# The MLP's down projection as seven block products (Strassen's scheme) in place of eight

## The chip, the cores and the metric

The kernel runs on one core of a Trainium2 chip. The metric is the time of one execution on the device, in microseconds (us). A run of a kernel gives several such times; the median is compared. Beside the times there is a profile of one execution, taken by the hardware profiler, with every instruction's start and length. The engines are TensorE (PE, with its weight loads as PEld), VectorE (DVE), ScalarE (ACT), GpSimd (POOL) and SyncE (SP), which here only issues transfers. Each engine works through its own queue in order and waits on semaphores of the others.

## What is computed

One layer of a streaming encoder on x of 512 tokens x 1024 channels, float32: four parallel token mixers, then cross-attention into 256 memory tokens, then a gated MLP. Only the MLP is touched:

```
hf  = rms_norm(x, norm_ffn_pre)                              # 512 x 1024
u   = dwconv_causal(hf @ w_up, ffn_dw) + ffn_dw_b            # w_up: 1024 x 5632, width-3 taps
u_g, u_v = split(u, 2, axis=-1)                              # 2816 channels each
yff = (silu(u_g) * u_v) @ w_down                             # w_down: 2816 x 1024
x   = x + rms_norm(yff, norm_ffn_post)
```

## The kernel before, in words

Every float32 product is made of three passes. Each operand is split into a high part, rounded to the type that PE multiplies in one pass (float32r), and a low part, the rest; `mm3` issues high x high, high x low, low x high into the same PSUM bank (line 224 is the `PE.matmul` that all of them share). A split is an ACT copy (the high part, L183 for weights, L152 for activations) and a DVE subtraction (the low part, L184 and L153).

Work is a stream of jobs, each a block of weights and a body that uses it. `run_blocks` keeps three jobs ahead: before it runs a body it fetches the next job, that is, it issues the load of the raw weights on SP (`load_raw`, L169, two raw tiles `wr` in turn) and their split into one of four pairs of tiles `wh` and `wl`. A planner then orders the instructions of each engine by a simulated time line, so the order in a queue can differ from the program's; what waits for what follows from the tiles.

Up projection (`up_jobs`): 44 blocks of 128 channels, gate and value block in turn, 24 matmuls each over all 512 tokens. The result lies channel by channel: 128 channels x 512 tokens in one of four PSUM banks (`mm`, `av`). `done` takes it out: scale and bias on ACT (L1286), two taps on DVE (L518), and after the value block the activation silu(gate) * value (L1290 to L1292). Before, that product is split into `ns.act`, a high and a low tile for all 22 channel blocks.

Down projection (`down_jobs`): 22 blocks `kk` of 128 channels. For each, 4 token tiles x 2 halves of the 1024 output columns, three passes each: the 128 x 128 activation is the stationary operand, 512 columns of `w_down` the moving one. The eight results fill the eight PSUM banks. The last four blocks are held back, and then done tile by tile: 12 matmuls close the first half of a token tile, 12 the second. Behind each half come a square with a sum on ACT (L1345) and a product with the gain on DVE (L1348); behind both, the reciprocal root of the mean square on POOL (`rstd_of`, L261 and L264), the residual sum on DVE (L1355) and the store to `out` on SP (L1356).

Of the kernel before, what the change touches and what calls it, by code (L numbers as in the profile page):

```python
# [16 lines left out]
F32 = mybir.dt.float32  # L17
F32R = mybir.dt.float32r
AF = mybir.ActivationFunctionType
ALU = mybir.AluOpType  # L20
# [4 lines left out]
P = 128  # L25
S = 512
D = 1024
NT = S // P
# [5 lines left out]
NF = DFF // P  # L34
EPS = 1e-6
WB = 2 * 520
# [46 lines left out]
def hybrid_layer(ctx: ExitStack, tc: tile.TileContext, a: dict, out: bass.AP):  # L83
    nc = tc.nc
    V, A, G, PE, SP = nc.vector, nc.scalar, nc.gpsimd, nc.tensor, nc.sync


    gp = ctx.enter_context(tc.tile_pool(name="g", bufs=1))
# [7 lines left out]
    def bank(tag=None):  # L96
        if tag is None:
            turn_of.n += 1
            tag = "av" if turn_of.shared and turn_of.n % 2 else "mm"
        return psum.tile([P, 512], F32, tag=tag, name=f"ps_{tag}", bufs=2)  # L100
# [41 lines left out]
    def weights_tile(kind):  # L142

        i = w_used[kind]
        w_used[kind] += 1
        return w_tiles.pop((kind, i), None) or gp.tile([P, WB], F32R, tag=f"{kind}{i % 4}", name=kind)


    def split(ps, hi, lo, scale=None):

        if scale is None:
            A.copy(hi, ps)  # L152
            V.tensor_tensor(lo, ps, hi.bitcast(F32), ALU.subtract)  # L153
        else:
            A.activation(hi, ps, AF.Copy if isinstance(scale, float) else AF.Identity, scale=scale)
            V.scalar_tensor_tensor(lo, ps, scale, hi.bitcast(F32), ALU.mult, ALU.subtract)
# [33 lines left out]
    def cols(w, c0, n=P, k0=0, nk=NK):  # L190

        return w[k0 * P:(k0 + nk) * P, c0:c0 + n].rearrange("(k p) c -> p k c", p=P), [P, nk, n]
# [3 lines left out]
    def run_blocks(jobs, ahead=3):  # L196


        jobs = iter(jobs)
        pending = []  # L200

        def fetch():
            while True:
                job = next(jobs, None)
                if job is None:
                    return
                if job[1] is None:
                    pending.append((job[0] or (), job[2]))
                else:
                    pending.append((load_weights(*job[:2], *job[3:]), job[2]))  # L210
                if job[0] is not None:
                    return

        for _ in range(ahead):
            fetch()
        while pending:
            if pending[0][0]:
                fetch()
            w, body = pending.pop(0)
            body(*w)  # L220
            bg.tick()
# [9 lines left out]
    def mm3(ps, w_hi, w_lo, x_hi, x_lo, first, last):  # L231

        matmul(ps, w_hi, x_hi, first, False)
        matmul(ps, w_hi, x_lo, False, False)
        matmul(ps, w_lo, x_hi, False, last)
# [20 lines left out]
    def rstd_of(pool, parts, n=1):  # L256

        m = pool.tile([P, n], F32, tag="st_m", name="st_m", bufs=4)
        r = pool.tile([P, n], F32, tag="st_r", name="st_r", bufs=4)
        if len(parts) == 2:  # L260
            G.tensor_scalar(m, parts[0], parts[1], EPS, ALU.add, ALU.add)  # L261
        else:
            G.tensor_scalar(m, parts[0], EPS, None, ALU.add)
        G.tensor_tensor(r, m, nhalf[:, :n], ALU.pow)  # L264
        return r
# [21 lines left out]
    def new_ht():  # L287
        if ht_tiles:
            return ht_tiles.pop(0), ht_tiles.pop(0)
        return (gp.tile([P, NK, S], F32R, tag="hth", name="hth"),  # L290
                gp.tile([P, NK, S], F32R, tag="htl", name="htl"))
# [973 lines left out]
            yield *cols(w_xo, b // 2 * 512, 512, b % 2 * 2, 2), body  # L1265


    def open_ffn():
        bg.drain("n1")
        close(ns.work_)  # L1270
        close(ns.xp_)
        close(ns.xm_)
        ns.fp_, ns.fp = new_pool("ffn", False)
        ns.work = ns.fp
        ns.act = (ns.fp.tile([P, NF, S], F32R, name="acth"), ns.fp.tile([P, NF, S], F32R, name="actl"))
        ns.post = ns.fp.tile([P, D], F32, name="g_ffn")
        G.dma_start(ns.post, a["norm_ffn_post"][0].partition_broadcast(P))

    def up_jobs():
        st, held = {}, []  # L1280

        def done(j, i, ps):
            if i == 0:
                st[j] = ns.fp.tile([P, 2, S], F32, tag="c", name="c", bufs=2)
            c, ch = st[j], i * NF + j
            A.activation(c[:, i], ps, AF.Identity, bias=pc("fb", ch), scale=pc("fdw2", ch))  # L1286
            taps(c[:, i], ps, lambda k: pc("fdw01", k * 44 + ch), 3)
            if i == 1:
                th = ns.fp.tile([P, S], F32, tag="th", name="th")
                A.activation(th, c[:, 0], AF.Tanh, scale=0.5)  # L1290
                V.scalar_tensor_tensor(th, th, 1.0, c[:, 0], ALU.add, ALU.mult)
                V.scalar_tensor_tensor(c[:, 1], th, 0.5, c[:, 1], ALU.mult, ALU.mult)  # L1292
                split(c[:, 1], ns.act[0][:, j], ns.act[1][:, j])


        for n in range(2 * NF):
            def body(hi, lo, n=n):
                j, i = divmod(n, 2)
                if n > 3:
                    ps = bank()  # L1300
                    channel_major(ps, (hi, lo), ns.hf)
                    done(j, i, ps)
                    return
                if n == 0:
                    bg.drain("n0")
                ps = bank(("mm", "sc")[n % 2])
                (channel_major if n else by_pass)(ps, (hi, lo), ns.hf, slice(0, S // 2))
                held.append((j, i, ps, (hi, lo)))
                if n == 3:
                    open_ffn()  # L1310
                    for j, i, ps, w in held:
                        (channel_major if i or j else by_pass)(ps, w, ns.hf, slice(S // 2, S))
                        done(j, i, ps)
            yield *cols(w_up, n % 2 * DFF + n // 2 * P), body, V, same, HALF_SHIFT if n < 4 else 0

    def down_jobs():
        tail = 4
        held, ps = [], []

        def step(t, i, kk, hi, lo):  # L1320
            sl, csl = slice(t * P, (t + 1) * P), slice(i * 512, (i + 1) * 512)
            mm3(ps[t][i], ns.act[0][:, kk, sl], ns.act[1][:, kk, sl], hi[:, csl], lo[:, csl], kk == 0, kk == NF - 1)

        for kk in range(NF):
            def body(hi, lo, kk=kk):
                if kk == 0:
                    tags = (("mm", "mm"), ("av", "av"), ("sc", "sc"), ("tr", "tr"))
                    ps.extend([bank(n) for n in pair] for pair in tags)
                if kk < NF - tail:
                    for t in range(NT):  # L1330
                        for i in range(2):
                            step(t, i, kk, hi, lo)
                    return
                held.append((kk, hi, lo))
                if kk < NF - 1:
                    return
                for t in range(NT):
                    res, o = ns.out[t], ns.fp.tile([P, 2, S], F32, tag="c", name="o", bufs=2)
                    ms = []
                    for i in range(2):  # L1340
                        for w in held:
                            step(t, i, *w)
                        ms.append(ns.fp.tile([P, 1], F32, tag=f"pm{i}", name=f"pm{i}", bufs=2))
                        junk = ns.fp.tile([P, S], F32, tag="th", name="junk")
                        A.activation(junk, ps[t][i], AF.Square, scale=1.0 / math.sqrt(D), accum_out=ms[i])  # L1345
                        if i == 1:
                            r = rstd_of(ns.fp, ms)
                        V.tensor_tensor(o[:, i], ps[t][i], ns.post[:, i * 512:(i + 1) * 512], ALU.mult)  # L1348
                    for i in range(2):
                        sl = slice(i * 512, (i + 1) * 512)  # L1350
                        parts = 2 if (t, i) == (NT - 1, 1) else 1
                        for q in range(parts):
                            n = 512 // parts
                            c, d = slice(q * n, (q + 1) * n), slice(sl.start + q * n, sl.start + (q + 1) * n)
                            V.scalar_tensor_tensor(o[:, i, c], o[:, i, c], r, res[:, d], ALU.mult, ALU.add)  # L1355
                            SP.dma_start(out[t * P:(t + 1) * P, d], o[:, i, c])  # L1356
            yield w_down[kk * P:(kk + 1) * P, :], [P, D], body

    def all_jobs():
        yield from mixer_jobs()  # L1360
# [43 lines left out]
```

## Time and profile before

| | |
|---|---|
| median of 3 runs | 1081.77 us (1080.86 to 1082.29) |
| profiled execution | 1081.09 us |
| its span, first to last instruction | 1079.3 us |
| PE busy | 1071.2 us, 99% of the span |
| up projection, the part with all its pools open | 728 to 953 us |
| down projection, first matmul to the last one's end | 953.17 to 1073.03 us |
| end after the last matmul | 6.27 us |
| matmuls in all | 5453 |

Lines of the profile name a group: the line of the kernel, the engine, the operation, what is written `<-` what is read with shapes, the count, the busy time and the mean of one instruction in nanoseconds, and the idle time of that engine just before, with what ended it. Rows of a time line give the start and the length in us first. Matmuls overlap in the pipeline, so their lengths add up to more than the time; their pace is read from their starts.

### The profile page before, as it was taken

The page shows a single profiled execution, that of the slowest core. Times are in us where ns is not written, and L with a number is a line of the kernel's source. Part 1 is how long each engine was busy: PE and PEld are TensorE (multiplying, and loading weights), DVE is VectorE, ACT ScalarE, POOL GpSimd, SP SyncE. Part 2 cuts the span into 40 slices and gives each one's busy share as a digit, 9 for nine tenths or more (in the row PEclk, how much of TensorE's full clock was granted, in tenths as well). Part 3 has the DMA queues.
Part 4 walks back from the last instruction along what each step waited for, and adds up shares of the span by engine and source line. Part 5 has one row for each costly group of instructions (what it writes and reads, how often), then busy time and mean ns, then how long its engine had stood idle before and what let it go on. Part 6 is the DMA issues. An engine that isn't in the chain of part 4 may idle for free.

```text
span 1079.3 us, 14199 instructions
## 1 busy us (share of the span) xinstructions
PE 1071.2 (99%) x5453; PEld 910.7 (84%) x5453; DVE 695.9 (64%) x1131; ACT 465.3 (43%) x785; POOL 104.0 (10%) x189
## 2 busy tenths in 40 slices
PE   9999999999999999999999999999999999999997
PEld 8888888888888988888888899998888888888886
DVE  7899996466666467857464486868666666642224
ACT  5322222467464364654443365645444444431112
POOL 4000001000101033323000120120000000000001
PEclk9999999999999999999999999999999999999999
DMA  6433433332222243233155343134333333333322
GB/s 203 116 98 91 90 107 95 93 98 78 59 81 78 69 127 98 81 96 117 59 176 180 113 146 92 57 99 118 97 98 98 98 98 98 98 98 97 98 78 78
DMA packets 145848, 109.29 MB, mean 101 GB/s; under 512 B 3647, under 2 KB 133292, under 8 KB 145781
## 3 DMA queue, kind: packets, MB, share of 16 engines
q1 hardware_dynamic: 143219, 99.85, 31.1%
q0 software_dynamic: 2560, 8.54, 2.7%
q8 instruction: 43, 0.70, 0.3%
q14 instruction: 24, 0.20, 0.1%
q10 hardware_dynamic: 2, 0.00, 0.0%
HBM read 106.27 MB, written 2.11 MB: 100 GB/s over the span
## 4 chain that ended last, share of the span: by engine, by line
PE 99%; ACT 0%; DVE 0%; POOLq 0%; issue 0%; DVEq 0%; POOL 0%; ACTq 0%
PE ps_mm L224 52%; PE ps_av L224 31%; PE ps_sc L224 8%; PE ps_tr L228 3%; PE ps_tr L224 3%; PE ps_mm L431 1%; PE ps_av L431 1%; PE ps_mm L373 0%; PE ps_sc L378 0%; DVE o L1355 0%; PE ps_tr L415 0%; POOLq L1400 0%; ACT junk L1345 0%; ACT hth L152 0%; ACT hth L421 0%
## 5 line engine op out<-in xcount | busy, mean ns | idle before, releaser
L184 DVE TENSOR_TENSOR wl<-wr,wh 128x1024 fp32r<-128x1024 f32 (+1 forms) x172 | 212.2, 1235 | 194.2 <-ACT wh L183 193.7
L183 ACT CAST wh<-wr 128x1024 fp32r<-128x1024 f32 (+1 forms) x172 | 180.1, 1049 | 318.4 <-PE ps_mm L224 127.8
L224 PE MATMUL ps_mm<-hth,wh 128*128 128x512 f32 (+1 forms) x616 | 231.4, 382 | 0.2 <-ACT hth L152 0.2
L224 PE MATMUL ps_mm<-hth,wl 128*128 128x512 f32 (+1 forms) x616 | 230.0, 380 | 0.0
L224 PE MATMUL ps_mm<-htl,wh 128*128 128x512 f32 (+1 forms) x616 | 229.9, 380 | 0.0
L224 PEld LDWEIGHTS ps_mm<-hth,wh 128*128 128x128 f32 x616 | 114.3, 188 | 21.1 <-ACT hth L152 0.5
L224 PEld LDWEIGHTS ps_mm<-hth,wl 128*128 128x128 f32 x616 | 114.0, 188 | 21.1
L224 PEld LDWEIGHTS ps_mm<-htl,wh 128*128 128x128 f32 x616 | 114.0, 188 | 20.4 <-DVE htl L153 0.2
L224 PE MATMUL ps_av<-hth,wh 128*128 128x512 f32 (+1 forms) x328 | 122.4, 373 | 0.0
L224 PE MATMUL ps_av<-htl,wh 128*128 128x512 f32 (+1 forms) x328 | 122.4, 373 | 0.0
L224 PE MATMUL ps_av<-hth,wl 128*128 128x512 f32 (+1 forms) x328 | 122.3, 373 | 0.0
L584 DVE SCALAR_TENSOR_TENSOR y<-y,par,y 128x499 f32<-128x499 f32 (+28 forms) x120 | 82.3, 729 | 0.2
L224 PEld LDWEIGHTS ps_av<-htl,wh 128*128 128x128 f32 x328 | 61.7, 188 | 10.9
L224 PEld LDWEIGHTS ps_av<-hth,wh 128*128 128x128 f32 x328 | 61.5, 188 | 10.9
L224 PEld LDWEIGHTS ps_av<-hth,wl 128*128 128x128 f32 x328 | 61.5, 188 | 10.8
L224 PE MATMUL ps_mm<-y,wh 128*128 128x512 f32 x192 | 61.2, 394 | 0.0
L261 POOL TENSOR_SCALAR st_m<-pm,pm 128x1 f32<-128x1 f32 x12 | 6.4, 533 | 435.6 <-ACT junk L1345 350.2
L224 PEld LDWEIGHTS ps_mm<-y,wh 128*128 128x128 f32 x192 | 35.4, 188 | 6.8
L152 ACT CAST acth<-c 128x512 fp32r<-128x512 f32 x22 | 13.7, 621 | 56.9 <-DVE c L1292 56.9
L224 PE MATMUL ps_mm<-y,wl 128*128 128x512 f32 x96 | 37.6, 392 | 0.0
L907 POOL TENSOR_SCALAR fbias<-ck,cq 128x128 f32<-128x128 f32 (+3 forms) x32 | 27.6, 868 | 68.0 <-DVE st L913 63.5
L518 DVE SCALAR_TENSOR_TENSOR c<-ps_mm,par,c 128x510 f32<-128x510 f32 (+1 forms) x44 | 32.8, 745 | 0.7
(379 smaller groups left out, 1901.4 us busy)
## 6 DMA issues: line engine op xcount, KB each, us to landing
wr<-in_w_up SPq DMA_DIRECT2D x44, 512.0 KB
wr<-in_w_in SPq DMA_DIRECT2D x38, 512.0 KB
wr<-in_w_gate SPq DMA_DIRECT2D x32, 512.0 KB
wr<-in_w_down SPq DMA_DIRECT2D x22, 512.0 KB
wr<-in_w_branch SPq DMA_DIRECT2D x16, 512.0 KB
wr<-in_w_out SPq DMA_DIRECT2D x8, 512.0 KB
xr<-in_w_xkv SPq DMA_DIRECT2D x8, 512.0 KB
wr<-in_w_in SPq DMA_DIRECT2D x4, 520.0 KB
```

The costliest lines, as they stand in the source:

```text
L152: A.copy(hi, ps)
L183: order(A.copy(hi, raw[:, :n]))
L184: low.tensor_tensor(lo, raw[:, :n], hi.bitcast(F32), ALU.subtract)
L224: PE.matmul(ps, lhs, rhs, start=start, stop=stop)
L228: PE.transpose(ps, x, ident[:n, :n])
L261: G.tensor_scalar(m, parts[0], parts[1], EPS, ALU.add, ALU.add)
L431: keep(PE.matmul(banks[c][:, :S // 2], w[p == 1][:, k, c * P:(c + 1) * P], ht[p == 2][:, i * 4 + k, :S // 2], start=(i, p, k) == (0, 0, 0) ...
L518: V.scalar_tensor_tensor(dst[:, s:], src[:, :S - s], w(k), dst[:, s:], ALU.mult, ALU.add)
L584: V.scalar_tensor_tensor(dst[:, s:], src[:, :S - s], pc("conv_dw", k * 4 + j), dst[:, s:], ALU.mult, ALU.add)
L907: G.tensor_scalar(bias[:, :w], ck[j][:, :w], -1.0, cq[:, qt, head:head + 1], ALU.mult, ALU.add)
```

## The change

The product Y = A B, with A the activations (512 tokens x 2816) and B = `w_down`, is cut into halves in each direction: A by tokens (first and last 256) and by channel blocks (even and odd ones), B by the same channel blocks and by its columns (first and last 512). So a pair `q` of channel blocks (2q, 2q + 1) gives A11, A12, A21, A22 (first index tokens, second even or odd block) and B11, B12, B21, B22, and there are 11 pairs. With Winograd's form of Strassen's scheme:

```
S1 = A21 + A22   S2 = S1 - A11   S3 = A11 - A21   S4 = A12 - S2
T1 = B12 - B11   T3 = B22 - B12  T2 = T3 + B11    N4 = B21 - T2
M1 = A11 B11   M2 = A12 B21   M3 = S4 B22   M4 = A22 N4   M5 = S1 T1   M6 = S2 T2   M7 = S3 T3
Y11 = M1 + M2              Y12 = M1 + M6 + M5 + M3
Y21 = M1 + M6 + M7 + M4    Y22 = M1 + M6 + M7 + M5
```

Each M sums over the 11 pairs in PSUM: 256 tokens x 512 columns, two banks.

- During the up projection, `weight_pair` (POOL's transfers) brings the two `w_down` blocks of a pair, `weight_sums` forms T3, T1, T2 and N4 on DVE in place, and POOL stores them in the DRAM tile `sums`. One pair comes every three blocks, from the seventh block on. The tiles are `dw`, four in turn.
- The activation is no longer split in the up projection. It is kept in float32 in `ns.quart[q]`, and after each odd block `activation_sums` makes S1, S3, S2, S4 of it on POOL, four sums of 256 columns.
- Phase 0 of the down projection: for each pair, job 0 loads B11 and T2 into one raw tile, job 1 T1 and T3; M1 and M6 are formed by the first, M5 and M7 by the second (12 matmuls each). [A11, S2, S1, S3] are split once for both. Eight banks are in use.
- `middle` empties the banks: M1 is copied to SBUF by ACT, DVE adds M6 to it, then M7 and M5, and finishes Y22 up to its gain.
- Phase 1: job 0 loads B21 and B22 for M2 and M3 (12 matmuls), job 1 N4 for M4 (6 matmuls). [A12, A22, S4] are split for both.
- The last four pairs of phase 1 are held, and `ends` closes M4 for two token tiles, then M2 and M3 for the first tile and for the second, 12 matmuls each, with a DVE sum from PSUM (`whole`) before the square and the gain product.
- Raw weights of the down projection go through the four `dw` tiles, with the load issued by the weights' own step. The splits of the activations go into the two `wr` tiles for the first pair, and afterwards into four slots of the tiles that held the up projection's input. `run_blocks` takes a job whose first part is a function and calls it when it fetches.

```diff
                 if job[1] is None:
-                    pending.append((job[0] or (), job[2]))
+                    pending.append((job[0]() if callable(job[0]) else job[0] or (), job[2]))
...
-        ns.act = (ns.fp.tile([P, NF, S], F32R, name="acth"), ns.fp.tile([P, NF, S], F32R, name="actl"))
+        ns.quart = [(ns.fp.tile([P, 4, S // 2], F32, tag=f"qa{q}", name="qa"),
+                     ns.fp.tile([P, 3, S // 2], F32, tag=f"qb{q}", name="qb")) for q in range(NF // 2)]
...
-                V.scalar_tensor_tensor(c[:, 1], th, 0.5, c[:, 1], ALU.mult, ALU.mult)
-                split(c[:, 1], ns.act[0][:, j], ns.act[1][:, j])
+                x = ns.quart[j // 2]
+                V.scalar_tensor_tensor(x[j % 2][:, 0:2].rearrange("p a b -> p (a b)"), th, 0.5, c[:, 1],
+                                       ALU.mult, ALU.mult)
+                if j % 2:
+                    activation_sums(*x)
...
                     done(j, i, ps)
+                    if n % 3 == 0 and n // 3 - 2 < NF // 2:
+                        weight_sums(n // 3 - 2)
+                        if n // 3 - 1 < NF // 2:
+                            weight_pair(n // 3 - 1)
...
+    def activation_sums(x, z):
+        G.tensor_tensor(x[:, 2], x[:, 1], z[:, 1], ALU.add)
+        G.tensor_tensor(x[:, 3], x[:, 0], x[:, 1], ALU.subtract)
+        G.tensor_tensor(x[:, 1], x[:, 2], x[:, 0], ALU.subtract)
+        G.tensor_tensor(z[:, 2], z[:, 0], x[:, 1], ALU.subtract)
+
+    def weight_pair(q):
+        ns.pair = [ns.fp.tile([P, D], F32, tag="dw", name="wp", bufs=4) for _ in range(2)]
+        for i in range(2):
+            G.dma_start(ns.pair[i], w_down[(2 * q + i) * P:(2 * q + i + 1) * P, :])
+
+    def weight_sums(q):
+        (b11, b12), (b21, b22) = ((x[:, :S], x[:, S:]) for x in ns.pair)
+        V.tensor_tensor(b22, b22, b12, ALU.subtract)
+        V.tensor_tensor(b12, b12, b11, ALU.subtract)
+        V.tensor_tensor(b11, b22, b11, ALU.add)
+        V.tensor_tensor(b21, b21, b11, ALU.subtract)
+        for i in range(2):
+            G.dma_start(sums[q * P:(q + 1) * P, i * D:(i + 1) * D], ns.pair[i])
...
+        def weights(phase, q, job):
+            n = 2 * (phase * pairs + q) + job
+            load(n + 3)
+            if job == 0:
+                activations(phase, q)
+            raw = raws[n]
+            if (phase, job) == (1, 1):
+                both = ns.fp.tile([P, D], F32R, tag=f"qa{q}", name="n4")
+                both = both[:, :half], both[:, half:]
+                split_to(*both, raw[:, :half])
+                return [both],
+            hi, lo = weights_tile("wh")[:, :D], weights_tile("wl")[:, :D]
+            split_to(hi, lo, raw)
+            return [(hi[:, i * half:(i + 1) * half], lo[:, i * half:(i + 1) * half]) for i in range(2)],
...
+        work = {(0, 0): (("M1", 0), ("M6", 1)), (0, 1): (("M5", 2), ("M7", 3)),
+                (1, 0): (("M2", 0), ("M3", 2)), (1, 1): (("M4", 1),)}
...
+            for t in range(2):
+                V.tensor_tensor(z7[:, t], u[:, t], banks["M7"][t], ALU.add)
+                V.tensor_tensor(u[:, t], u[:, t], banks["M5"][t], ALU.add)
+            for t in range(2):
+                V.tensor_tensor(z[:, t], u[:, t], banks["M7"][t], ALU.add)
+            for t in range(2):
+                ms[2 + t, 1] = square(z[:, t], 1)
+                V.tensor_tensor(z[:, t], z[:, t], ns.post[:, gains[1]], ALU.mult)
...
+            def whole(name, t, x, pieces=1):
+                for c in range(pieces):
+                    cut = slice(c * S // pieces, (c + 1) * S // pieces)
+                    for q, job, ws in held:
+                        for (n, a), w in zip(work[1, job], ws):
+                            if n == name:
+                                step(name, t, q, a, w, 1, cut)
+                    V.tensor_tensor(x[:, cut], x[:, cut], banks[name][t][:, cut], ALU.add)
+                return x
+
+            for t in range(2):
+                x = whole("M4", t, z7[:, t])
+                finish(2 + t, {1: z[:, t], 0: x}, result(2 + t, 0, x, x))
+            for t in range(2):
+                x = whole("M2", t, m1[:, t])
+                result(t, 0, x, x)
+                x = whole("M3", t, u[:, t])
+                finish(t, {0: m1[:, t], 1: x}, result(t, 1, x, x))
+
+        def body(phase, q, job, ws):
+            if (phase, q, job) == (0, 0, 0):
+                for name, tag in (("M1", "sc"), ("M6", "tr"), ("M5", "mm"), ("M7", "av")):
+                    banks[name] = [bank(tag) for _ in range(2)]
+            if (phase, q, job) == (1, 0, 0):
+                for name, tag in (("M2", "sc"), ("M3", "tr"), ("M4", "mm")):
+                    banks[name] = [bank(tag) for _ in range(2)]
+            if phase and q >= pairs - hold:
+                held.append((q, job, ws))
+                if (q, job) == (pairs - 1, 1):
+                    ends()
+                return
+            for (name, a), w in zip(work[phase, job], ws):
+                for t in range(2):
+                    step(name, t, q, a, w, phase)
+            if (phase, q) == (0, pairs - 1):
+                middle(job)
```

More of the change, by code (lines that the diff above doesn't have):

```diff
@@ L1265, in cross_out_jobs @@
             yield *cols(w_xo, b // 2 * 512, 512, b % 2 * 2, 2), body
+    sums = dram.tile([NF // 2 * P, 2 * D], F32, name="sums")
     def open_ffn():
@@ L1313, in body @@
                         done(j, i, ps)
+                    weight_pair(0)
             yield *cols(w_up, n % 2 * DFF + n // 2 * P), body, V, same, HALF_SHIFT if n < 4 else 0
-    def down_jobs():
[L1317 to L1357, printed above, removed]
```

85 lines of the change are left out of this document (added).

## The prediction

> **What bounds the kernel now.** I read the page first (busy shares, slices, the chain that ended last), then the waits of TensorE (PE), then busy times by stage, and last the rows of the stage that is rewritten.
>
> ```profile
> span 1079.3 us, 14199 instructions
> PE 1071.2 (99%) x5453; PEld 910.7 (84%) x5453; DVE 695.9 (64%) x1131; ACT 465.3 (43%) x785; POOL 104.0 (10%) x189
> PE   9999999999999999999999999999999999999997
> PEclk9999999999999999999999999999999999999999
> PE 99%; ACT 0%; DVE 0%; POOLq 0%; issue 0%; DVEq 0%; POOL 0%; ACTq 0%
> ```
> PE is the chain, from the first slice to the last, at full clock. The waits of PE from 30 to 1070 us say whether anything ever holds it up:
>
> ```profile
> engine line waited for: us in total, times, longest us
> PE ps_mm L224 <- ACT hth L152: 0.2, 1, 0.2
> ```
> One wait of 0.2 us in 1040 us, across every change of stage. Only fewer matmuls, a shorter end, or a new wait can change the time. The next table gives the busy time of each engine in the up projection (728 to 953 us), in the down projection, and in the end after the last matmul (number of instructions in brackets, then clock, DMA share and GB/s). The two rows below it are the first and the last matmul of the down projection.
>
> ```profile
> core 0: us, PE busy (x) PEld busy (x) DVE busy (x) ACT busy (x) POOL busy (x), PEclk, DMA share, GB/s
> 0.00:10.00 10.00, 8.68 (x28) 5.69 (x29) 5.73 (x12) 3.93 (x7) 4.78 (x15) 1.00 0.85 278
> 10.00:20.00 10.00, 9.76 (x86) 9.52 (x84) 7.83 (x9) 7.10 (x12) 7.10 (x8) 1.00 0.71 230
> 728.00:953.00 225.00, 225.00 (x1029) 187.60 (x1028) 156.40 (x193) 100.94 (x129) 0.00 (x0) 1.00 0.34 101
> 953.17:1073.03 119.86, 119.85 (x529) 98.91 (x527) 35.05 (x36) 26.03 (x35) 2.59 (x6) 1.00 0.28 88
> 1073.03:1079.30 6.27, 0.00 (x0) 0.00 (x0) 2.23 (x4) 0.69 (x2) 0.86 (x2) 0.71 0.23 84
> ...
> 953.17 0.39 PE L224 MATMUL ps_mm<-wh,acth 128*128 128x512 f32 x1
> 1072.63 0.39 PE L224 MATMUL ps_tr<-wh,actl 128*128 128x512 f32 x1
> ```
>
> **The matmuls.** Before: 22 channel blocks x 4 token tiles x 2 column halves x 3 passes = 528 matmuls of 512 columns (the row's 529 counts one that overlaps its edge). First to last start is 1072.63 - 953.17 = 119.46 us over 527 steps: 0.2267 us each; the 0.39 us shown is the overlapped length, not the pace. After: 7 products x 11 pairs x 2 token tiles x 3 passes = 462 matmuls, of the same shape (stationary 128x128 activation, moving 512 columns of weight). So 66 fewer: **-14.96 us**. The Trainium skill (TensorE: Matmul & The Clock Gate, "What happens when you issue a matmul") puts a stream of such matmuls at 215.7 ns; by it the saving would be 14.2 us. The trace has 226.7 ns here, and that decides.
>
> **What PE hands to the others in the down projection.** A pair of channel blocks took 48 matmuls, 10.88 us, and two weight splits. Now phase 0 has 24 matmuls (5.44 us) and phase 1 has 18 (4.08 us) a pair. Prices of the elementwise work, from the down stage and the up projection:
>
> ```profile
> L184 DVE TENSOR_TENSOR wl<-wr,wh 128x1024 fp32r<-128x1024 f32 x19 | 23.3, 1225 | 73.9 <-ACT wh L183 73.9
> L183 ACT CAST wh<-wr 128x1024 fp32r<-128x1024 f32 x19 | 19.9, 1049 | 76.1 <-PE ps_tr L224 71.2 <-PE ps_av L224 4.9
> L153 DVE TENSOR_TENSOR actl<-c,acth 128x512 fp32r<-128x512 f32 x21 | 14.5, 691 | 13.1 <-ACT acth L152 13.1
> L518 DVE SCALAR_TENSOR_TENSOR c<-ps_av,par,c 128x511 f32<-128x511 f32 x19 | 14.3, 750 | 0.7
> L1286 ACT ACTIVATE c<-ps_av,par 128x512 f32<-128x512 f32 x19 | 14.7, 773 | 0.0
> L1290 ACT ACTIVATE th<-c 128x512 f32<-128x512 f32 x22 | 13.9, 631 | 41.1 <-DVE c L518 41.1
> L1348 DVE TENSOR_TENSOR o<-ps_sc,g_ffn 128x512 f32<-128x512 f32 x2 | 1.4, 691 | 2.3 <-ACT junk L1345 2.3
> ```
> Phase 0, a pair: two weight splits and one activation split of 1024 columns. DVE 3 x 1.225 = 3.68 us, ACT 3 x 1.049 = 3.15 us, in 5.44 us. Phase 1: one weight split of 1024, n4 of 512, activations of 768 (between 0.69 and 1.225, say 0.96). DVE 1.225 + 0.69 + 0.96 = 2.88 us in 4.08 us. Both fit, at about 70%, and splits are issued three jobs ahead of PE. Cost 0; the cover is those three jobs, up to 8 us of matmuls.
>
> **Start of the down projection.** The activations of pair 1 go into the tiles that hold the up projection's input, free only after its last matmul. Their split, 1.05 + 1.225 us, stands beside the last block's evacuation on ACT and DVE, 0.77 + 2 x 0.75 us first and three operations of 0.6 to 0.7 us behind them. PE has the 24 matmuls of pair 0 meanwhile, whose operands wait in the freed raw tiles. If that cover went, 2.3 us would show; I take 0.
>
> **Loads in the down projection.** SP moves 512 KB per job in phase 0 and 512 + 256 KB per pair in phase 1: 11 x 1.75 MB (MB of 1024 x 1024 bytes) = 20.2 million bytes in 104.7 us, 193 GB/s, against 88 before. The first two rows of the table show 278 and 230 GB/s at shares of 0.85 and 0.71, so about 325 at full share: the engines would be 60% busy. The harder limit is the ring of four raw tiles. Landing times of SP's loads are not shown; POOL's loads of the same 512 KB are the nearest rows:
>
> ```profile
> xin<-in_x POOLq DMA_DIRECT2D x4, 512.0 KB, 4.2
> g_mem<-in_norm_mem POOLq DMA_DIRECT2D x1, 512.0 KB, 5.9
> g_ffn<-in_norm_ffn_post POOLq DMA_DIRECT2D x1, 512.0 KB, 4.0
> ```
> A raw tile is refilled when its split ends: 2.4 us (ACT then DVE), up to 3.7 with an activation split in front. With a landing of 4.0 to 5.9 us a turn is 6.4 to 9.6 us. PE uses four jobs in 10.88 us. Cost 0, with 1.3 us or more to spare. SP has nothing else to do between loads; its output issues come after them, as before.
>
> **The up projection.** Removed per channel block: one ACT copy of 512 columns and the DVE subtraction of 0.69 us. Added per pair: four DVE sums of 512 columns (0.69 us each, 11 x 4 = 44), four POOL sums of 256 columns (44), two loads and two stores of 512 KB issued by POOL. DVE in the 225 us window: 156.4 - 14.5 + 30.4 = 172.3 us, 77%. The DVE sums wait for loads that were issued three blocks (72 matmuls, 16.3 us) earlier and land in 4 to 6 us; should they wait after all, the next weight's subtraction is queued behind them on DVE, and PE has three blocks of split weights before it notices. The stores wait in POOL's queue for the DVE sums; behind them stand the next loads, with 16 us, and the activation sums, wanted no earlier than phase 0. DMA adds 44 x 512 KB = 23 million bytes over about 190 us: 101 rises to some 220 GB/s, below the 278 seen. PSUM has four banks in turn, so an evacuation may be late by three blocks too. Cost 0.
>
> POOL's sums have no row of their own size. POOL here: a sum of 512 columns is 1.32 us; a scalar operation of 256 columns is 0.79 us, of 512 columns 1.17 us.
>
> ```profile
> L404 POOL TENSOR_TENSOR wa<-e,wa x4: 1291/1320/1350, 8.2 to 13.7; 128x512 fp32r<-128x512 f32 x4
> L907 POOL TENSOR_SCALAR fbias<-ck,cq 128x256 f32<-128x256 f32 x8 | 6.3, 789 | 26.6 <-DVE st L913 26.5
> L907 POOL TENSOR_SCALAR fbias<-ck,cq 128x512 f32<-128x512 f32 x8 | 9.3, 1171 | 24.6 <-DVE st L913 24.6
> L184 DVE TENSOR_TENSOR wl<-wr,wh x172: 1207/1225/2009, 14.1 to 1052.4; 128x1024 fp32r<-128x1024 f32 x168, 128x1040 fp32r<-128x1040 f32 x4
> 12.46 2.61 POOL L404 TENSOR_TENSOR wa<-e,wa 128x512 fp32r<-128x512 f32 x2
> 14.14 3.14 DVE L184 TENSOR_TENSOR wl<-wr,wh 128x1024 fp32r<-128x1024 f32 x2 [0.26 <-ACT wh L183]
> ```
> A POOL sum is then 0.79 to 1.32 us; scaled as its neighbours, 1.32 x 0.79 / 1.17 = 0.89 us, 39 us in all. The last two rows show what that can do: two subtractions starting at 14.14 take 3.14 us, where 2.45 is usual, and the one of 2.01 us lies across the end of a POOL sum at 15.07. If every POOL sum held DVE for its whole length, DVE would have 172.3 + 39 = 211 us in 225: still under. The Trainium skill (SBUF — State Buffer, "SBUF: two separate sides") says that GpSimd and a VectorE operation with two SBUF inputs exclude each other for a whole instruction. The 2.01 us agree with it. It is the second rival's mechanism.
>
> **Between the phases.** Two ACT copies and ten DVE operations (0.69 us each) take M1, M6, M5 and M7 out of their banks. M2 and M3 need only M1's and M6's banks, and those are emptied (two copies, two sums) while PE does M5 and M7 of the last pair, 2.72 us. M4 needs M5's banks: four DVE operations after the last M5 and M7 matmuls, 2.8 us and some 0.3 for the matmul's end. PE has 12 matmuls of M2 and M3 (2.72 us) and the first of M4's two banks to fill before it wants the second, at 3.4 us. In that order nothing is lost; with the next job's subtractions in front (1.225 + 0.96) M4 would wait 1.9 us; with no splits in hand at all, the eight DVE operations would show: 5.5 us. I take **+0.7**: the trace shows every other stage change at 0.2 or less, but this one has less cover. Bounds 0 and 5.5.
>
> **The end.** PE closes M4, M2, M3 tile by tile, 12 matmuls each (2.72 us), against 24 before. Per closed tile DVE has a sum, a gain product and up to two residual operations, 2.8 us at most, at times half of that, so it keeps up. After the last matmul the chain was:
>
> ```profile
> 1073.11 0.60 ACT L1345 ACTIVATE junk<-ps_tr 128x512 f32<-128x512 f32 x1 [2.01 <-PE ps_tr L224]
> 1073.90 0.30 POOL L261 TENSOR_SCALAR st_m<-pm,pm 128x1 f32<-128x1 f32 x1 [4.49 <-ACT junk L1345]
> 1074.29 0.56 POOL L264 TENSOR_TENSOR st_r<-st_m,nhalf 128x1 f32<-128x1 f32 x1
> 1074.88 1.54 DVE L1355 SCALAR_TENSOR_TENSOR o<-o,st_r,res 128x512 f32<-128x512 f32 x3 [0.36 <-POOL st_r L264]
> ```
> It stays as it is behind one new DVE sum of 0.69 us plus a hand-over of about 0.1: **+0.8**. Bounds 0.7 and 2.1 (with a preceding pair of DVE operations in the way).
>
> **The sum.** The profiled execution took 1081.09 us, 0.68 under the median 1081.77. 1081.09 - 14.96 + 0.7 + 0.8 = 1067.6; against the median **1068.3 us**, 1.2% faster. Bounds of these terms together: 1081.77 - 14.96 + 0.7 = 1067.5 to 1081.77 - 14.96 + 5.5 + 2.1 + 2.3 = 1076.7.
>
> **The rivals.**
> *The ring of loads starves the down projection (slower).* For it: twice the bytes per matmul, two transfers per raw tile, and pairs of sums read back from DRAM. Against it: 278 GB/s seen, and a spare of 1.3 us. It decides once a landing passes 10.88 - 2.4 = 8.5 us; the gain is gone once the turn is 12.3 us. At a landing of 10 us the turn is 12.4, and 20.2 / 2.1 = 9.6 turns take 119 us in place of 105: +14.5, so 1083 us.
> *POOL's sums hold up DVE in the up projection.* It needs more than 225 us of DVE. At 0.89 us a sum it does not; at 1.32 us (58 us of POOL, 230 of DVE) PE loses 5 us: about 1074 us.
> *The change of phase costs what its upper bound says.* 5.5 us and some of the start's 2.3: about 1074 us.
> *It does not do what it says.* If the pace fell so that 462 matmuls take as long as 528 (0.259 us each), nothing is gained: 1082. The shapes are the same, so there is little for it.
>
> **How the numbers follow.** The forecast (1067 to 1071) 0.65; phase change or start at their bounds 0.15; POOL against DVE 0.09; the ring, slower 0.08; no gain 0.03. Two tenths of a per cent (2.2 us) are what a measurement here can tell from no change. So faster 0.89, same 0.03, slower 0.08. The range goes from 1066.3 (the lower bound less the scatter of the runs) to 1077 (the upper bound); it leaves out the ring and the null, and a tail of the others.
>
> **What would show it.** Right: 5387 matmuls, the down projection 104 to 106 us long at 0.2267 us a matmul, DMA near 193 GB/s in it, no PE wait of over 2 us, a sum in front of the last square. Wrong: PE waits on a split that itself waits for a load (the ring); PE idle before 940 us behind a DVE subtraction (POOL against DVE); PE waits on DVE for M4's banks at the change of phase; a granted clock under 1.0 after such gaps.

## The result, and the profile after

| | before | after |
|---|---|---|
| median of 18 runs each | 1081.18 us (1080.42 to 1083.36) | 1078.09 us (1075.48 to 1081.40) |
| ratio to before, 95% interval | | 0.997 (0.9959 to 0.998) |
| span of the profiled execution | 1079.3 us | 1078.4 us |

The kernel is 0.3% faster; 1.2% was forecast, and the time lies above the range of 1066.3 to 1077 us. Its executions differ by up to 6 us, and the profiled one (1080.23 us) is 2.1 us above the median: the parts named below add up to its span, not to the median. The lines of the page after that answer to those of before (busy time by engine; two of the 40-slice rows; the chain that ended last, by engine):

```profile
span 1078.4 us, 14440 instructions
PE 1058.9 (98%) x5387; PEld 899.4 (83%) x5387; DVE 758.1 (70%) x1211; ACT 488.5 (45%) x809; POOL 172.7 (16%) x277
DMA  6433433332222243233255343146889843226662
GB/s 203 117 98 91 90 105 95 94 98 78 59 81 79 63 134 98 79 98 115 62 176 173 120 139 97 59 154 215 268 285 292 269 118 98 79 78 192 215 189 78
...
PE 85%; DMA 7%; DVE 3%; issue 2%; POOL 1%; ACT 1%; POOLq 0%; DVEq 0%; ACTq 0%
```

The 66 matmuls are gone, but PE is no longer the whole chain: transfers and DVE stand in it. The slices say where to look. From the 28th to the 32nd (some 728 to 863 us) the transfers run at 215 to 292 GB/s, and then fall back to 118 and less for the rest of the up projection. They should have been spread over the whole up projection. Busy times of each engine by stage (same columns as before: the crowded part in two stretches, four microseconds in it, the down projection, the end):

```profile
core 0: us, PE busy (x) PEld busy (x) DVE busy (x) ACT busy (x) POOL busy (x), PEclk, DMA share, GB/s
735.00:800.00 65.00, 65.00 (x293) 53.96 (x292) 51.56 (x70) 22.63 (x30) 24.95 (x34) 1.00 0.80 257
800.00:850.00 50.00, 43.67 (x184) 35.14 (x183) 37.77 (x51) 14.76 (x19) 16.71 (x26) 0.97 0.90 289
846.00:850.00 4.00, 3.81 (x10) 3.09 (x11) 3.29 (x5) 0.55 (x1) 3.20 (x4) 0.57 0.76 201
962.13:1066.82 104.69, 104.69 (x462) 86.54 (x461) 81.57 (x89) 61.65 (x79) 6.83 (x9) 1.00 0.54 168
1066.82:1078.40 11.58, 0.39 (x2) 0.00 (x0) 4.45 (x8) 0.72 (x2) 1.98 (x3) 0.70 0.25 91
...
962.13 0.39 PE L225 MATMUL ps_sc<-wh,wr 128*128 128x512 f32 x1
1066.82 0.39 PE L225 MATMUL ps_tr<-wh,hth 128*128 128x512 f32 x1
```

Three marks, the same in both kernels, split the difference of the spans:

| | before | after | difference |
|---|---|---|---|
| first matmul of the down projection | 953.17 | 962.13 | +8.96 |
| from there to the start of the last matmul | 119.46 | 104.69 | -14.77 |
| from there to the end | 6.67 | 11.58 | +4.91 |
| span | 1079.3 | 1078.4 | -0.9 |

The down projection gives what was forecast, with no wait of PE in it. The up projection, untouched in its matmuls, takes 9 us more; the end takes 5 more.

**The up projection.** What PE waited for between 735 and 850 us, and what DVE and ACT waited for (us in total, times, longest):

```profile
PE ps_mm L225 <- DVE c L519: 3.8, 2, 2.3
PE ps_av L225 <- DVE c L519: 2.5, 1, 2.5
...
DVE wp L1351 <- DMA wp<-in_w_down: 14.1, 5, 4.8
...
ACT wh L183 <- DMA wr<-in_w_up: 33.3, 10, 7.0
```

PE waits three times for a PSUM bank that DVE has not emptied (L519 are the taps). Those evacuations were not late by themselves: DVE had stood at the first sum of a weight pair (L1351), whose load had not landed. So it is at each of the three waits, with 2.12, 2.74 and 4.79 us of standing. The first and the last of them, in the rows of DVE, PE and POOL's transfers:

```profile
809.14 0.69 DVE L1351 TENSOR_TENSOR wp<-wp 128x512 f32<-128x512 f32 x1 [2.12 <-DMA wp<-in_w_down]
...
813.63 0.47 PE L225 MATMUL ps_mm<-hth,wh 128*128 128x512 f32 x1 [1.50 <-DVE c L519]
...
831.60 0.54 POOL L1346 DMA_DIRECT2D wp<-in_w_down  x1 [4.49 <-DMA sums<-wp]
833.37 0.54 POOL L1346 DMA_DIRECT2D wp<-in_w_down  x1 [1.23 <-DMA sums<-wp]
...
834.06 1.52 DVE L519 SCALAR_TENSOR_TENSOR c<-ps_mm,par,c 128x510 f32<-128x510 f32 x2
840.37 0.69 DVE L1351 TENSOR_TENSOR wp<-wp 128x512 f32<-128x512 f32 x1 [4.79 <-DMA wp<-in_w_down]
...
842.91 1.22 DVE L184 TENSOR_TENSOR wl<-wr,wh 128x1024 fp32r<-128x1024 f32 x1
844.04 0.74 DVE L519 SCALAR_TENSOR_TENSOR c<-ps_av,par,c 128x510 f32<-128x510 f32 x1
...
845.30 0.75 DVE L519 SCALAR_TENSOR_TENSOR c<-ps_av,par,c 128x511 f32<-128x511 f32 x1
...
846.19 0.76 PE L225 MATMUL ps_av<-hth,wh 128*128 128x512 f32 x1 [2.51 <-DVE c L519]
...
847.17 0.63 PE L225 MATMUL ps_av<-hth,wl 128*128 128x512 f32 x1
847.60 0.63 PE L225 MATMUL ps_av<-hth,wh 128*128 128x512 f32 x1
```

In the last of them DVE stands 4.79 us, then works off sums and a subtraction, and the bank is free 2.51 us too late. Behind that wait the matmuls step at 0.43 us (847.17 to 847.60) for about 3.5 us: the granted clock was 0.57 between 846 and 850. So this wait cost some 1.7 us more than its length. By the starts of PE's matmuls the three waits and the slow steps make 8.5 of the 8.96 us. The Trainium skill (TensorE: Matmul & The Clock Gate, "Part 1: The HAM clock gate (the 'warmup' mystery)") puts the fall to half the clock behind an idle window of about 3.4 us. Here 2.5 us of waiting were enough; the measurement decides. The waits of 1.5 and 2.3 us before it were not followed by slow steps.

Why was the load late? The sums' first line by count and by first and last start, in this kernel:

```profile
L1351 DVE TENSOR_TENSOR wp<-wp x11: 675/691/824, 731.8 to 840.4; 128x512 f32<-128x512 f32 x11
```

The code writes one pair behind every third block, 16.3 us apart. The planner orders by what its model takes as ready, and nothing ties a sum to its block; so it set all eleven pairs as early as their tiles allowed, 11 us apart, in the first half of the up projection. Their transfers met there. The load of the last pair was issued at 831.60 and 833.37, each time only when an earlier store of the same tile had landed, and the sum that needs it was next in DVE's queue from 835.58 on. Over the eleven pairs POOL waited 35.8 us for such stores. So these loads were issued late first of all; landing took 6.2 us at the median, where 4 to 6 were assumed.

**The end.** The last closing, in time order:

```profile
1066.82 0.39 PE L225 MATMUL ps_tr<-wh,hth 128*128 128x512 f32 x1
...
1067.48 0.75 DVE L1476 SCALAR_TENSOR_TENSOR wr<-wr,st_r,res 128x512 f32<-128x512 f32 x1 [0.46 <-POOL st_r L265]
...
1068.81 0.68 DVE L1491 TENSOR_TENSOR o<-o,ps_tr 128x512 f32<-128x512 f32 x1
1069.58 0.63 ACT L1428 ACTIVATE junk<-o 128x512 f32<-128x512 f32 x1 [3.28 <-DVE o L1491]
...
1070.34 0.69 DVE L1467 TENSOR_TENSOR o<-o,g_ffn 128x512 f32<-128x512 f32 x1 [0.85 <-ACT junk L1428]
1070.40 0.80 POOL L262 TENSOR_SCALAR st_m<-pm,pm 128x1 f32<-128x1 f32 x1 [2.96 <-ACT junk L1428]
...
1071.88 0.75 DVE L1476 SCALAR_TENSOR_TENSOR wr<-wr,st_r,res 128x512 f32<-128x512 f32 x1 [0.85 <-POOL st_r L265]
1072.54 0.87 DVE L1476 SCALAR_TENSOR_TENSOR o<-o,st_r,res 128x256 f32<-128x256 f32 x2
```

Four parts make the 4.91 us. The last sum starts 1.99 us behind the last matmul's start, where the square, first in line before the change, started 0.48 us behind it: DVE was still at the tile before, +1.5. The sum and its hand-over: 1069.58 (the square) - 1068.81, +0.8. POOL's step takes 0.80 us in place of 0.30, beside a product that now has two SBUF inputs: +0.5. And from DVE's last instruction (1073.41) to the end pass 4.99 us, where it was 2.88: +2.1. That last part is POOL's closing drain, the row DRAIN at the end of its queue (shortest, median and longest of three; first of before, then of after):

```profile
L1400 POOLq DRAIN  x3: 40/93/2817, 1074.2 to 1079.0; - x3
```
```profile
L1567 POOLq DRAIN  x3: 40/102/6411, 1071.2 to 1078.2; - x3
```

### The profile page after: what moved, and what is told of

Same layout as the page of the kernel before. It is cut to its first block, busy times and chain, and to the rows that moved or that the text cites. A ratio compares the mean times of both kernels' runs of the same rounds, so it can differ in the third digit from the quotient of the medians.

```text
span 1078.4 us, 14440 instructions
## 1 busy us (share of the span) xinstructions
PE 1058.9 (98%) x5387; PEld 899.4 (83%) x5387; DVE 758.1 (70%) x1211; ACT 488.5 (45%) x809; POOL 172.7 (16%) x277
## 4 chain that ended last, share of the span: by engine, by line
PE 85%; DMA 7%; DVE 3%; issue 2%; POOL 1%; ACT 1%; POOLq 0%; DVEq 0%; ACTq 0%
PE ps_mm L225 45%; PE ps_av L225 25%; PE ps_sc L225 7%; DMA sums<-wp 4%; PE ps_tr L229 3%; PE ps_tr L225 2%; DMA wp<-in_w_down 2%; DVE wl L184 1%; PE ps_mm L432 1%; ACT wh L183 0%; DVE c L519 0%; PE ps_av L432 0%; PE ps_mm L374 0%; DMA wr<-in_w_gate 0%; DMA wr<-in_w_in 0%
## 5 line engine op out<-in xcount | busy, mean ns | idle before, releaser
L183 ACT CAST wh<-wr 128x1024 fp32r<-128x1024 f32 (+1 forms) x150 | 156.9, 1048 | 289.0 <-PE ps_mm L225 140.3
L184 DVE TENSOR_TENSOR wl<-wr,wh 128x1024 fp32r<-128x1024 f32 (+1 forms) x150 | 186.0, 1242 | 112.8 <-ACT wh L183 112.4
L225 PEld LDWEIGHTS ps_av<-htl,wh 128*128 128x128 f32 x328 | 62.1, 189 | 10.8
L1379 DVE TENSOR_TENSOR wl<-dw,wh 128x1024 fp32r<-128x1024 f32 x33 | 41.4, 1260 | 13.4 <-ACT wh L1378 13.3
L1378 ACT CAST wh<-dw 128x1024 fp32r<-128x1024 f32 x33 | 34.5, 1052 | 23.2 <-PE ps_tr L225 8.4
L1294 ACT ACTIVATE th<-c 128x512 f32<-128x512 f32 x22 | 13.9, 632 | 62.4 <-DVE c L519 59.7
```

Of the source, the lines that this page charges most:

```text
L183: order(A.copy(hi, raw[:, :n]))
L184: low.tensor_tensor(lo, raw[:, :n], hi.bitcast(F32), ALU.subtract)
L225: PE.matmul(ps, lhs, rhs, start=start, stop=stop)
L1378: A.copy(hi, x)
L1379: V.tensor_tensor(lo, x, hi.bitcast(F32), ALU.subtract)
```

## The experiments

Three of the profiled executions below lost time between 395 and 405 us, in the mixers that the change does not touch: about 1.7 us with both edits, 4 with bare transfers, 3 with products apart. For these three the stages are compared, not the spans. The runs belong to three batches, in which the kernel before had medians of 1084.52 (the first four experiments), 1081.35 (bare transfers, products apart, transfers on SP, all four) and 1080.97 us (the loose sums); a difference of 0.3% between ratios of different batches says nothing.

### Sums in their places (e1_paced)

```diff
-        V.tensor_tensor(b22, b22, b12, ALU.subtract)
+        keep(V.tensor_tensor(b22, b22, b12, ALU.subtract))
```
`keep` pins an instruction behind the one written before it on its engine.

> The changed kernel with one edit: the first DVE sum of each weight pair stays behind the evacuation of the block that it is written after, so that a pair comes every three blocks (16.3 us) and not as early as its tiles allow. All work is still done. Theory A (the sums were pulled to the front of the up projection, where transfers crowd; DVE stands at a late one, the evacuation behind it is late, PE waits and its clock drops): the up projection ends at 953 to 954 us of the span in place of 962.3, PE does not wait in it, 1069 us, 9 less than the changed kernel. Theory B (DVE, POOL and DMA simply have too much to do in the up projection, wherever it stands): it stays at 1076 to 1079 us.

Measured: 1071.22 us (1071.18 to 1071.65), ratio to before 0.9886 (0.9866 to 0.9907). The sums by first and last start, and the same two stretches as above:

```profile
L1351 DVE TENSOR_TENSOR wp<-wp x11: 679/683/686, 755.9 to 919.4; 128x512 f32<-128x512 f32 x11
...
735.00:800.00 65.00, 65.00 (x293) 53.98 (x293) 52.36 (x66) 25.80 (x32) 18.33 (x25) 1.00 0.61 193
800.00:850.00 50.00, 50.00 (x222) 41.39 (x221) 40.32 (x49) 18.27 (x23) 15.31 (x21) 1.00 0.70 223
```
PE is busy throughout, with the same sums, stores and loads; the down projection begins at 953.59. The last load of a pair is issued at 897.1, 22 us ahead of the sum that needs it (919.4); in the changed kernel it was 7 us (833.37 and 840.37). DVE did more work in these 115 us than in the changed kernel (92.7 against 89.3 us). Theory A holds; that there is too much to do (B) falls. The gain was 7 and not 9 us by the medians; by the profiled executions it is 8.5. This edit spreads the transfers and takes away DVE's waits at once; which of the two counts is asked further down.

### Closing matmuls in their written order (e2_ends)

```diff
-        PE.matmul(ps, lhs, rhs, start=start, stop=stop)
+        ins = PE.matmul(ps, lhs, rhs, start=start, stop=stop)
+        if pin.on:
+            keep(ins)
...
             m1, u, z7, z = (parts[n] for n in ("m1", "u", "z7", "z"))
+            pin.on = True
```
The last two lines stand in `ends`.

> The changed kernel with one edit: the matmuls that close M4, M2 and M3 are kept in the order in which they are written, tile by tile. All work is still done. Theory A for the end (PE closes both tiles of M4 late and all seven closings fall into its last 10 us, so DVE works them off after PE): the end after the last matmul falls from 11.6 us to about 7, DVE has its first sum of the end some 2.7 us after the held matmuls begin, 1074 us. Theory B (DVE has more work at the end than PE, in any order): no change, 1078 us.

Measured: 1077.04 us, ratio 0.994 (0.9919 to 0.9962). From the last matmul's start (1064.19) to the end (1075.0) it is 10.8 us in place of 11.6, so 0.8 us and not the 4.6 expected. Theory A for the end falls as it was put: M4's first tile does close some 4 us ahead of the second, but DVE still waits in its own queue, up to 0.85 us for ACT's square before a product and as much for POOL's root.

### Both (e3_both)

The two edits together.

> Both edits together: the weight sums stay in their places and the closing matmuls in theirs. All work is still done. If both theories A hold the two gains add: 1064 to 1066 us, which is 15 to 17 less than the kernel before. If only the first holds 1069, if only the second 1074, if neither 1078.

Measured: 1072.17 us (1070.83 to 1073.90), ratio 0.9895 (0.9872 to 0.9918): by the medians, as with the sums in their places alone. By the stages the end is 10.8 us in place of 11.6 again (1060.04 to 1070.8), and the 1.7 us that this execution lost in the mixers hide it. The expectation missed by 6 us, because the first gain was 7 us and not 9, the second 0.8 and not 4.

### No weight sums (e4_nosums)

`weight_pair` and `weight_sums` are not called; the down projection loads blocks of `w_down` in place of `sums`.

> The changed kernel without the pairs' loads, the DVE sums and their stores in the up projection; the down projection reads blocks of the weights of the same sizes in place of the sums, so the output is not the MLP's. The POOL sums of the activations stay. Theory A: this is all that the up projection lost: it ends at 953 us, 1069 us, the same as the paced kernel within 1 us. If POOL's sums hold up DVE, the up projection still ends late, and the time is over 1071 us.

Measured: 1069.58 us, ratio 0.9869 (0.9845 to 0.9894); the down projection begins at 953.29. POOL's activation sums stay in this kernel, as they do beside the weight sums in the paced one, and PE does not wait in the up projection of either, so the second rival of the prediction falls. The rest against the paced kernel, 1.6 us, is the shorter drain (below).

### Transfers alone, as crowded (e5_transfers)

```diff
-        V.tensor_tensor(b22, b22, b12, ALU.subtract)
-        V.tensor_tensor(b12, b12, b11, ALU.subtract)
-        V.tensor_tensor(b11, b22, b11, ALU.add)
-        V.tensor_tensor(b21, b21, b11, ALU.subtract)
```

> The changed kernel without the 44 DVE sums of the weights; each pair is loaded and stored again as it is, so the output is not the MLP's. The transfers still come as early as their tiles allow. Theory A1 (what costs the 9 us is DVE standing at a sum whose load is late, with evacuations queued behind it): no DVE wait on a pair's load is left, the up projection ends at 953 to 955 us of the span, about 1070 us. Theory A2 (the crowded transfers themselves delay the up projection's own weights, and DVE stands at the low part of such a weight): ACT still waits for these weights, some 30 us in all, PE still waits, and the up projection ends after 957 us, 1074 us or more.

Measured: 1071.26 us, ratio 0.9899 (0.9879 to 0.9919).

```profile
735.00:800.00 65.00, 65.00 (x310) 54.62 (x309) 43.67 (x55) 25.33 (x32) 26.00 (x41) 1.00 0.99 342
800.00:850.00 50.00, 50.00 (x222) 41.44 (x221) 31.62 (x38) 21.11 (x26) 10.84 (x18) 1.00 0.77 246
...
ACT wh L183 <- DMA wr<-in_w_up: 34.1, 12, 6.2
```
Even more crowded (342 GB/s), ACT waits as long for the up projection's own weights as in the changed kernel (34 us), and PE does not wait in the up projection. The down projection begins at 957.25, with the 4 us of the mixers in it. A1 holds and A2 falls, except that there is less work on DVE here. The next run closes that.

### As crowded, with as much DVE work that waits for no load (e9_loose)

```diff
-        V.tensor_tensor(b22, b22, b12, ALU.subtract)
...
+        d = ns.quart[-1][0][:, 2:4].rearrange("p a b -> p (a b)")
...
+        keep(V.tensor_tensor(d, d, d, ALU.subtract))
+        for _ in range(3):
+            V.tensor_tensor(d, d, d, ALU.add)
```

> The changed kernel with its transfers as early and as crowded as before, but the 44 DVE sums of the same size work on a spare tile, not on what is loaded, four behind every third block's evacuation; the pairs are stored as they were loaded, so the output is not the MLP's. DVE has the same work and never waits for a pair's load. Theory A1 (DVE standing at a late pair is what reaches PE): no PE wait in the up projection, it ends at 953 to 955 us of the span, 1071 us. Theory A3 (crowded transfers and this much DVE work suffice together): PE waits for evacuations in the crowded part, over 1 us in all, 1073 us or more.

Measured: 1071.18 us, ratio 0.9914 (0.9896 to 0.9932); the down projection begins at 953.21.

```profile
735.00:800.00 65.00, 65.00 (x292) 53.91 (x291) 44.64 (x57) 22.52 (x28) 24.61 (x39) 1.00 0.94 319
800.00:850.00 50.00, 50.00 (x222) 41.42 (x221) 40.66 (x52) 21.19 (x27) 13.50 (x17) 1.00 0.79 251
...
ACT wh L183 <- DMA wr<-in_w_up: 41.8, 14, 7.1
```
Crowded transfers, late weights (41.8 us) and the DVE work together (85.3 us in these two stretches, 89.3 in the changed kernel) do not reach PE. A3 falls as it was put. What is left is DVE standing at a pair that has not landed, which the rows of the changed kernel show ahead of each wait of PE. The DVE work is spread here, as in the paced kernel; sums as early as in the changed kernel that wait for nothing were not tried, so that their crowding has a share is not ruled out.

### Products in tiles of their own (e6_apart)

On top of the paced sums:

```diff
-                finish(2 + t, {1: z[:, t], 0: x}, result(2 + t, 0, x, x))
+                y = apart()
+                finish(2 + t, {1: z[:, t], 0: y}, result(2 + t, 0, x, y))
```
and so for M2 and M3; `apart` gives a free `qa` tile.

> The kernel with the paced sums, and the gain products of the end written to tiles of their own and no longer over what ACT squares. All work is still done. Theory A (at the end DVE is the queue that everything waits in, and 0.85 us of each closing is DVE waiting for ACT's square before it may overwrite): the last sum starts 0.5 us after the last matmul and not 2.0, the last square's POOL step is 0.3 us and not 0.8, because the product no longer runs beside it; 2 us less than the paced kernel, 1069 us. Theory B (only the order of the queue counts, DVE's waits move elsewhere): under 0.5 us.

Measured: 1070.74 us, ratio 0.9895 (0.9875 to 0.9915), 0.5 less than the paced kernel by the medians, which is within the scatter.

```profile
1061.47 0.39 PE L225 MATMUL ps_tr<-wh,hth 128*128 128x512 f32 x1
...
1063.80 0.68 DVE L1495 TENSOR_TENSOR o<-o,ps_tr 128x512 f32<-128x512 f32 x1
...
1065.39 0.30 POOL L262 TENSOR_SCALAR st_m<-pm,pm 128x1 f32<-128x1 f32 x1 [2.96 <-ACT junk L1428]
```
POOL's step of the last closing is back at 0.30 us, half a microsecond less. But the last sum starts 2.3 us behind the last matmul, not 2.0, so the end is 11.4 us long (1072.9 - 1061.47) in place of 11.6: with PE's order as the planner has it, DVE is at residual sums of the tile before. Theory A is right in the POOL step alone, B in the rest.

### Transfers on SP (e7_sp)

On top of the paced sums:

```diff
-            G.dma_start(ns.pair[i], w_down[(2 * q + i) * P:(2 * q + i + 1) * P, :])
+            SP.dma_start(ns.pair[i], w_down[(2 * q + i) * P:(2 * q + i + 1) * P, :])
...
-            G.dma_start(sums[q * P:(q + 1) * P, i * D:(i + 1) * D], ns.pair[i])
+            SP.dma_start(sums[q * P:(q + 1) * P, i * D:(i + 1) * D], ns.pair[i])
```

> The kernel with the paced sums, and the pairs' 44 loads and stores issued by SP in place of POOL. All work is still done. Theory A (POOL's closing drain is longer by 3.6 us because POOL issued 44 transfers more, and 1.7 us of it show at the end): the drain falls from 6.4 to 2.8 us, as before the change, 1069.5 us. If SP's queue, where a store now waits for its sums ahead of the next weights, held up the up projection, PE would wait in it and the time would be over 1071 us. Theory B (the drain is longer for another reason): it stays 6.4 us, 1071 us.

Measured: 1070.28 us (1068.56 to 1072.61), ratio 0.9893 (0.9868 to 0.9917). The scatter is as wide as the expected gain, so the profile decides:

```profile
L1567 POOLq DRAIN  x3: 40/93/2816, 1062.2 to 1067.1; - x3
```
The drain is back at 2.8 us, the span 1067.3 against 1069.9, and PE does not wait in the up projection. From DVE's last instruction to the end it is 2.9 us again.

### All four (e8_all)

Sums in their places, closing matmuls in theirs, products apart, transfers on SP; all work is done.

> All four edits: paced sums, closing matmuls in their written order, products in tiles of their own, transfers on SP. All work is still done. If the parts add: 14.96 us for the matmuls, less 0.8 for the new sum at the end, less 0 to 1 for what is left of DVE's queue: 1066 to 1068 us. If the end is still DVE's: 1069 us.

Measured: **1067.15 us** (1066.40 to 1067.60), ratio to before 0.9862 (0.9845 to 0.9879), faster than both kernels. Its last matmul and what follows, and its chain by engine:

```profile
1057.67 0.39 PE L226 MATMUL ps_tr<-wh,hth 128*128 128x512 f32 x1
1058.10 0.69 DVE L1499 TENSOR_TENSOR o<-o,ps_tr 128x512 f32<-128x512 f32 x1
1058.88 0.63 ACT L1431 ACTIVATE junk<-o 128x512 f32<-128x512 f32 x1 [0.81 <-DVE o L1499]
1059.70 0.30 POOL L265 TENSOR_SCALAR st_m<-pm,pm 128x1 f32<-128x1 f32 x1 [4.49 <-ACT junk L1431]
1060.68 1.54 DVE L1483 SCALAR_TENSOR_TENSOR gp<-gp,st_r,res 128x512 f32<-128x512 f32 x3 [1.16 <-POOL st_r L268]
...
PE 99%; DVE 0%; ACT 0%; POOLq 0%; issue 0%; DVEq 0%; POOL 0%; ACTq 0%
```
The last matmul starts at 1057.67, 14.96 us ahead of that of before, 1072.63. DVE takes its sum 0.43 us later, and the end is 7.4 us long (1065.1 - 1057.67), 0.8 more than before. Against the kernel with SP's transfers alone the end is 2.1 us shorter (9.5 to 7.4), where the closing order alone gave 0.8 and products apart 0.2: DVE's queue clears only with both. The forecast's time is reached with these edits alone; the kernel that was forecast did not have them.

## Why the prediction was wrong, step by step

- **The matmuls: right.** -14.96 us forecast, -14.77 measured over the down projection. The last kernel's is 104.68 us long, -14.78; that its last matmul comes 14.96 us earlier, to the digit of the forecast, is chance, for its down projection began 0.18 us earlier.
- **Weight and activation splits, the ring of loads, the start of the down projection: right.** 0 forecast; PE has no wait there. The transfers ran at 168 GB/s and not at 193; some of the stage's loads were issued before it, from 841.88 us on. The slower rival (the ring) did not come.
- **Between the phases: a little high.** +0.7 forecast, at most 0.2 measured: 104.69 us against 461 steps of 0.2267, which make 104.5.
- **The up projection: wrong, and this is the step that failed.** It was put at 0 because "the DVE sums wait for loads that were issued three blocks (72 matmuls, 16.3 us) earlier and land in 4 to 6 us", and transfers were averaged over 190 us to 220 GB/s. Both took the order of the code for the order on the chip, although the kernel's planner moves whatever is not tied. The pairs came 11 us apart, transfers ran at 257 to 289 GB/s, loads were issued only when the stores of their tiles had landed, the last one 7 us before its sum started and not 16.3, and DVE stood for 14 us with evacuations behind it. The sentence on what is queued behind a waiting sum named the weights' subtraction and three blocks of cover; the evacuation of PSUM was the one that failed, for +8.96 us in the profiled execution, some 1.7 of it through the clock. The paced kernel shows that with the assumed order the term is 0.4.
- **The end: the mechanism was right, the size was not.** +0.8 forecast for a new sum, which is what that sum cost. Left out were DVE's backlog (+1.5; "so it keeps up" counted its work and not its waits for ACT and POOL inside each closing, and here too PE's closings were not in the written order, which gave 0.8 back), POOL's step beside a product with two SBUF inputs (+0.5), and POOL's drain (+2.1), for which nothing in the trace of before gave a sign that it would grow.
- **The rivals.** The one on POOL and DVE named the stage and the engine that held PE up, but for a cause that did not make PE wait in the paced kernel. Single rows in the up projection show it (a weight sum of 1.11 us in place of 0.69, at 822.17, beside a POOL sum), and so does the end. The bounds had no place for an order other than the written one, so the range ended at 1077.

## What to carry to other kernels

Where a planner orders the instructions, "issued three blocks ahead" is a wish until a dependency or a pinned order makes it so: look for work that is ready early and tie its first instruction to the place where its cover is. A load that is late costs little on an engine whose next work can also wait (ACT stood 34 to 42 us here without a wait of PE); it costs much on the one that empties PSUM. And at the end of a kernel, count an engine's waits inside each closing with its work, for there is nothing behind to hide them.

## What the runs showed of the hardware

- POOL's drain at the end of the program took 2.81 to 2.82 us where POOL had not issued the pairs' transfers (before, without sums, transfers on SP, all four), and 6.41 us in the kernels where it had issued these 44 more. Some 2 us of that showed. What in the count sets it was not tried.
- Some waits of PE were followed, at once or within about 2 us, by some 3.4 us of matmuls at 0.43 us a step in place of 0.2267, about half the clock. It was so behind waits of 2.5 us (changed kernel), 1.9 us (closing order), and 1.8 and 1.6 us (bare transfers and products apart, in the mixers). It was not so behind 1.5 and 2.3 us (changed kernel), 3.0 us (closing order) and 1.6 us (both edits, in the mixers). So the length of the wait alone does not decide it; what else does, no run shows.
- A POOL operation on one column took 0.80 us in place of 0.30 while DVE worked on two SBUF operands, and 0.30 again when the product ran ahead of it. The Trainium skill (SBUF — State Buffer, "SBUF: two separate sides") has a lock between such a DVE instruction and a GpSimd one that reads SBUF; these rows agree with it.
